# Reading a gate/up pair only when both are summed, with one w_down group between any two blocks

## The chip, the cores and the metric

The kernel runs on one core of a Trainium2 chip. The metric is the device time of one execution in microseconds (us), taken as the median of the runs. Engines are named as in the profile: PE multiplies matrices (PEld loads its stationary operand), DVE and ACT do elementwise work, POOL does a little of it, SP issues the transfers from memory.

## What is computed

One decoder layer on 256 tokens of width 2048, all in float32: a half-step feed-forward block, a mixer (sparse attention next to latent attention), and a second half-step feed-forward block. The change touches only the two feed-forward blocks:

```
def swiglu(x, w_gate, w_up, w_down):
    return (jax.nn.silu(x @ w_gate) * (x @ w_up)) @ w_down

h = rms_norm(x, ffn1_norm[l])
x = x + 0.5 * swiglu(h, ffn1_w_gate[l], ffn1_w_up[l], ffn1_w_down[l])
...
h = rms_norm(x, ffn2_norm[l])
x = x + 0.5 * swiglu(h, ffn2_w_gate[l], ffn2_w_up[l], ffn2_w_down[l])
```

w_gate and w_up are 2048 x 5632, w_down is 5632 x 2048.

## The kernel before

**Products.** Each float32 product is made of three products of a shorter format. A weight tile raw is split into w_hi (a rounding copy on ACT, line 470) and w_lo (a subtraction on DVE, line 478); mm3 (line 290) then issues high x high, high x low and low x high into the same sums.

**Parts.** Weights come as tiles of 1 MB, three of which can be in flight (RAW, line 28), and are split in parts of 1024 columns (the last part of a w_down tile has 512). Five parts may be split ahead of the one that PE is multiplying (SPLIT, line 28): the cast of a part can start when PE has finished with the part five places earlier, whose buffer it takes.

**Feed-forward work.** The 5632 hidden columns are 44 blocks of 128, in chunks of 6, 6, 6, 6, 6, 6, 4, 4 (CHS, line 22). A block is 96 matmuls of 256 columns: two parts of w_gate (q 0 and 1), two parts of w_up (q 2 and 3), 24 matmuls each. Gate goes to one half of a PSUM bank and up to the other half of the same bank (halves, line 650). Blocks of the first chunk take banks 4 and 5 in turn (ps_s); all later ones take bank 7 alone (ps_u, BANKS on line 30). A group of w_down products is called "D" in the plan: four parts, 7 x 3 = 21 matmuls of 512 columns into banks 0 to 6 (ps_m). It uses a scheme with seven products where eight would be direct, so DVE also adds weights (tsum, lines 461 to 466) and activations (lines 623 to 625). The groups of chunk k-1 are spread among the blocks of chunk k. The last chunk's w_down is multiplied directly after the last block ("L", ps_acc).

**Activation.** swish (line 591) takes a block from PSUM: DVE multiplies gate by the norm factor rb (ff_g), ACT takes tanh (ff_t), DVE finishes the silu (ff_g again) and multiplies by up, read from PSUM (asum). After every second block a pair is formed: three small DVE operations, a cast on ACT and a subtraction on DVE (act). Once all blocks of a chunk have met one half of w_down, the seven sums are added to a tile in SBUF (sum<-ps_m, turnover on line 653); after the last chunk but one, combine (line 667) folds them into x.

**Order.** Every engine runs its instructions in the order in which they were written out. go (line 212) writes that order at build time with a clock of its own for PE, DVE and ACT: dense work is one stream, and the activation steps are side jobs that step when their inputs are due by that clock. Waits between engines are put in from the tiles that each instruction reads and writes; a PSUM bank is one such tile. plan (line 331) sets how blocks and groups of w_down follow one another. Counted in PE's order, in chunks 1 to 5 and 7 a group of 21 matmuls stands before each block of 96. (Chunks are numbered from 0.) Chunk 6 has 4 blocks and 6 groups, and its matmuls between groups are 48, 72, 72, 48, 72, 72: two of its blocks follow another without a group between.

Of the kernel before, what the change touches and what calls it, by code (L numbers as in the profile page):

```python
# [7 lines left out]
F32 = mybir.dt.float32  # L8
# [6 lines left out]
P = 128  # L15
T = 256
# [6 lines left out]
FROM = [sum(CHS[:k]) for k in range(len(CHS))]  # L23
# [7 lines left out]
NEVER = 1e9  # L31
# [125 lines left out]
class _Layer:  # L157
# [32 lines left out]
        self.ev[key] = max([self.pe.clk] + [self.when(x) for x in aps])  # L190

    def at(self, *keys):
        return lambda: max(self.ev.get(k, NEVER) for k in keys)

    def fresh(self, *aps):
        return max(self.when(x) for x in aps)
# [134 lines left out]
    def plan(self):  # L331

        seq, way = [], 1
        for k, n in enumerate(CHS):
            gs = [("G", k, i, q) for i in range(0 if k else 2, n) for q in range(4)]
            if not k:
                seq += [("F", 0, 0, 0)] + gs
                continue
            ds = [("D", k - 1, g, j) for g in range(2)[::way] for j in range(CHS[k - 1] // 2)]
            way = -way  # L340
            for i, d in enumerate(ds):

                a, b = (len(gs) * x // len(ds) for x in (i, i + 1))
                if n >= len(ds):
                    a, b = (x // 4 * 4 for x in (a, b))
                seq.append(d)
                seq += gs[a:b]

        seq += [("L", LAST, 2 * g + i, q) for g in range(NG // 2) for q in range(CHS[LAST] // 2) for i in range(2)]
        return seq  # L350
# [234 lines left out]
    def ffn(self, ap, h, ssq, after, first):  # L585
        key, gain = ("f1", G_FFN1) if first else ("f2", G_FFN2)
# [4 lines left out]
        def swish(banks, pg, pu, k, i):  # L591

            n, (j, m) = FROM[k] + i, divmod(i, 2)
            yield self.at("rb" + key, *([("act", key, n - 2)] if n > 1 else []))
            yield self.fresh(pg)
            g, t = (ap.tile([P, T], F32, name=f"ff_{x}", tag=f"ff_{x}", bufs=2) for x in "gt")
            V.tensor_mul(g, pg, self.rb)
            S.activation(t, g, AF.Tanh, scale=0.5)
            yield self.fresh(t)
            V.scalar_tensor_tensor(g, t, 1.0, g, op0=ALU.add, op1=ALU.mult)  # L600
            yield self.at(("up", key, n), *([("act", key, n - 1)] if n else []))
            if m == 0:
                if n:
                    yield self.at(("pair", key, n // 2 - 1))
                raw[j] = ap.tile([P, 8, P], F32, name="asum", tag="asum")
            yield self.fresh(pu)

            r = raw[j]
            if k == LAST:
                dst = r[:, 2 * m:2 * m + 2]  # L610
            else:
                dst = r[:, 0:3:2] if m else r[:, 1:8:6]
            V.tensor_mul(dst, g.rearrange("p (a t) -> p a t", a=2), pu.rearrange("p (a t) -> p a t", a=2))
            self.leave(*banks)
            self.mark(("act", key, n), dst)
            if not m:
                return
            yield self.fresh(r)
            if k == LAST:
                f, r = acts[k][:, j, :, :4], r[:, :4]  # L620
            else:
                f = acts[k][:, j]
                V.tensor_sub(r[:, 3:5], r[:, 7:8].to_broadcast([P, 2, P]), r[:, 1:3])
                V.tensor_sub(r[:, 5], r[:, 1], r[:, 4])
                V.tensor_sub(r[:, 6], r[:, 0], r[:, 5])
                r = r[:, :7]
                yield self.fresh(r)
            S.copy(f[:, 0], r)
            yield self.fresh(f[:, 0])
            V.tensor_sub(f[:, 1], r, f[:, 0].bitcast(F32))  # L630
            self.mark(("form", key, k, j), f)
            self.mark(("pair", key, n // 2))
# [67 lines left out]
        def dense():  # L700
# [7 lines left out]
            for what, k, i, q in plan:  # L708
                if what == "F" or (what, i, q) == ("G", 0, 0):
                    acts[k] = ap.tile([P, 3, 2, 7, P], F32R, name="act", tag="act", bufs=2)  # L710
                if what == "F":
                    yield self.slot("acc", 4)
                    pb = [self.bank("acc")[:, :T] for _ in range(4)]
                    c = 0
                    while c < C:
                        yield self.at(*(("h", gain, x) for x in range(c, c + self.coming() // 512)))
                        w = self.take(P)
                        for j in range(w[0].shape[1] // 4):
                            for b in range(4):
                                self.mm3(pb[b], [x[:, 4 * j + b] for x in w], (h[:, c, 0], h[:, c, 1]), c == 0, c == C - 1)  # L720
                            c += 1
                            if j + 1 < w[0].shape[1] // 4:
                                yield
                        self.n_used += 1
                        yield
                    for b in range(2):
                        self.mark(("up", key, b))
                        self.spawn(swish(pb[2 * b:2 * b + 2], pb[2 * b], pb[2 * b + 1], 0, b))
                elif what == "G":
                    if q == 0:  # L730
                        yield self.slot("u" if k else "s", 1)
                        p = self.bank("u" if k else "s")
                    m, half = divmod(q, 2)
                    w = self.take(P)
                    for c in range(8):
                        cc = half * 8 + c
                        self.mm3(halves(p)[:, m], [x[:, c] for x in w], (h[:, cc, 0], h[:, cc, 1]), cc == 0, cc == C - 1)
                        if c in FINE:
                            yield
                    self.n_used += 1  # L740
                    yield
                    if q == 1:
                        self.spawn(swish([p], halves(p)[:, 0], halves(p)[:, 1], k, i))
                    if q == 3:
                        self.mark(("up", key, FROM[k] + i))
                elif what == "D":
                    if first and k == 0 and q == 0:
                        for g in (2 * i, 2 * i + 1):
                            self.fetch(self.columns(g), self.a["xt"][g])
                            self.mark(("x", g), self.columns(g))  # L750
                    new = q == 0 and (k == 0 or was[k, i][1] != i)
                    if new:
                        banks = {}
                    yield self.at(("form", key, k, q))
                    f = acts[k][:, q]
                    to = nxt.get((k, i))
                    end = q == CHS[k] // 2 - 1 and (to is None or to[1] != i)

                    for sums in (((1, 0), (6, 2)), ((0, 1), (3, 5)), ((4, 3), (5, 4)), ((2, 6),)):
                        if new:  # L760
                            for l, o in sums:
                                yield self.slot("m", 1)
                                banks[o] = self.bank("m")
                        w = self.take(512)
                        for j, (l, o) in enumerate(sums):
                            self.mm3(banks[o], (f[:, 0, l], f[:, 1, l]), [x[:, j] for x in w], new, end)
                        self.n_used += 1
                        yield
                    if end:
                        self.spawn(turnover(banks, k, i, (k, i) in began), 2)  # L770
                else:
                    if q == 0:
                        yield self.slot("acc", 2)
                        last[i] = [self.bank("acc"), self.bank("acc")]
                    p = last[i]
                    w = self.take(512)
                    yield self.at(("form", key, k, q))
                    f = acts[k][:, q]
                    for j in range(2):
                        for tb in range(2):  # L780
                            self.mm3(p[tb], (f[:, 0, 2 * j + tb], f[:, 1, 2 * j + tb]), (w[0][:, j], w[1][:, j]),
                                     q + j == 0, q + 1 == CHS[k] // 2 and j == 1)
                            if tb + j < 2:
                                yield
                    self.n_used += 1
                    yield
                    if q + 1 == CHS[k] // 2:
                        self.spawn(added(p, i))
# [786 lines left out]
```

## Time and profile before

| | us |
|---|---|
| median of 3 runs | 2023.28 (2023.16 to 2024.9) |
| the profiled execution | 2023.27 |
| its span, first to last instruction | 2021.5 |
| PE busy | 1865.4 (92%) |
| DVE busy | 1514.9 (75%) |
| ACT busy | 986.6 (49%) |
| first feed-forward block | about 0 to 830 |
| mixer | about 830 to 1225 |
| second feed-forward block | about 1225 to 2021 |

A row of the timeline gives start, length, engine, line, operation and tile, and in brackets the idle time before it and what ended that. Matmuls overlap, so a matmul's length is longer than the distance to the next one; the distance between starts is what counts. PEclk is the granted clock of PE, 1.00 at full rate. An execution is 1.77 us longer than its span.

### The profile page before, as it was taken

What the parts mean: (1) busy time and instruction counts of PE and PEld (TensorE: products, weight loads), DVE (VectorE), ACT (ScalarE), POOL (GpSimd) and SP (SyncE); (2) the same over time, 40 slices, a digit from 0 to 9 for tenths busy, and PEclk for the clock granted to TensorE, in tenths of its full rate; (3) what the DMA queues carried; (4) which work ended last, traced back from release to release, by engine and by line L of the source; (5) the groups of instructions that cost most, each with busy time, mean ns of one, the idle gap of its engine ahead of it and who ended that gap; (6) DMA issues with size and microseconds to landing.
All of it is one profiled execution on the core that took longest, in us unless ns stands there. A gap on an engine that the chain in (4) does not pass through costs nothing.

```text
span 2021.5 us, 30343 instructions
## 1 busy us (share of the span) xinstructions
PE 1865.4 (92%) x12157; PEld 1693.5 (84%) x12157; DVE 1514.9 (75%) x2272; ACT 986.6 (49%) x1289; POOL 101.0 (5%) x232
## 2 busy tenths in 40 slices
PE   7999999998999888899979999999989989999988
PEld 7988888888888788788867789898988888888887
DVE  7677777778777779776667765776778777778787
ACT  4454554444445444554555554454544544444442
POOL 6000000000000000101013200000000000000000
PEclk9999999999999899999989999999999999999999
DMA  6455554455445444475322454444554445445443
GB/s 234 171 195 194 179 193 153 163 188 177 157 167 185 148 176 158 158 269 207 130 97 85 148 186 167 167 175 159 188 188 167 167 167 188 166 154 182 166 167 125
DMA packets 54941, 344.29 MB, mean 170 GB/s; under 512 B 6544, under 2 KB 8592, under 8 KB 16912
## 3 DMA queue, kind: packets, MB, share of 16 engines
q1 hardware_dynamic: 54800, 342.36, 48.2%
q8 instruction: 95, 1.56, 0.3%
q14 instruction: 46, 0.38, 0.1%
HBM read 340.24 MB, written 2.10 MB: 169 GB/s over the span
## 4 chain that ended last, share of the span: by engine, by line
PE 68%; DVE 22%; issue 3%; ACT 3%; POOL 2%; DMA 1%; SPq 0%; ACTq 0%; POOLq 0%; DVEq 0%
PE ps_u L273 33%; PE ps_m L273 14%; PE ps_acc L273 12%; DVE w_lo L133 9%; PE ps_s L273 7%; DVE tsum L133 3%; ACT w_hi L133 2%; DVE ff_g L133 2%; DVE act L133 2%; DVE sum L133 2%; DVE asum L133 2%; DVE raw L133 1%; PE ps_t L273 1%; PE ps_t L288 1%; DVE x L133 1%
## 5 line engine op out<-in xcount | busy, mean ns | idle before, releaser
L273 PE MATMUL ps_u<-h,w_hi 128*128 128x256 f32 x4864 | 908.1, 289 | 106.0 <-DVE ff_g L133 103.5
L133 DVE TENSOR_TENSOR w_lo<-raw,w_hi 128x1024 fp32r<-128x1024 f32 (+4 forms) x645 | 773.8, 1215 | 256.0 <-ACT w_hi L133 254.8
L133 ACT CAST w_hi<-raw 128x1024 fp32r<-128x1024 f32 (+4 forms) x645 | 661.1, 1039 | 538.4 <-PE ps_u L273 199.4
L273 PEld LDWEIGHTS ps_u<-h,w_hi 128*128 128x128 f32 x4864 | 781.1, 196 | 128.3 <-DVE ff_g L133 118.0
L273 PE MATMUL ps_u<-h,w_lo 128*128 128x256 f32 x2432 | 698.5, 287 | 5.0 <-DVE w_lo L133 5.0
L273 PEld LDWEIGHTS ps_u<-h,w_lo 128*128 128x128 f32 x2432 | 477.4, 196 | 5.4 <-DVE w_lo L133 5.4
L273 PE MATMUL ps_m<-w_hi,act 128*128 128x512 f32 x1120 | 365.8, 396 | 0.0
L133 ACT CAST w_hi<-tsum 128x1024 fp32r<-128x1024 f32 (+1 forms) x160 | 133.4, 833 | 255.1 <-PE ps_u L273 226.6
L273 PEld LDWEIGHTS ps_m<-w_hi,act 128*128 128x128 f32 x1120 | 210.8, 188 | 47.7
L133 DVE TENSOR_TENSOR w_lo<-tsum,w_hi 128x1024 fp32r<-128x1024 f32 (+1 forms) x160 | 151.6, 953 | 111.0 <-ACT w_hi L133 111.0
L273 PE MATMUL ps_m<-w_lo,act 128*128 128x512 f32 x560 | 221.9, 396 | 0.0
L273 PEld LDWEIGHTS ps_m<-w_lo,act 128*128 128x128 f32 x560 | 105.3, 188 | 22.0
L273 PE MATMUL ps_acc<-w_hi,h 128*128 128x512 f32 (+2 forms) x384 | 119.8, 381 | 0.0
L133 DVE TENSOR_TENSOR tsum<-tsum,raw 128x512 f32<-128x512 f32 x160 | 109.2, 683 | 0.1
L133 ACT ACTIVATE ff_t<-ff_g 128x256 f32<-128x256 f32 x88 | 36.7, 420 | 134.1 <-DVE ff_g L133 134.1
L273 PE MATMUL ps_s<-h,w_hi 128*128 128x256 f32 x512 | 93.5, 285 | 4.2 <-DVE ff_g L133 4.2
L273 PEld LDWEIGHTS ps_s<-h,w_hi 128*128 128x128 f32 x512 | 80.0, 192 | 5.8 <-DVE ff_g L133 5.0
L273 PEld LDWEIGHTS ps_acc<-w_hi,h 128*128 128x128 f32 x384 | 71.2, 188 | 12.4 <-issue 1.6
L273 PE MATMUL ps_acc<-h,w_hi 128*128 128x256 f32 (+1 forms) x320 | 73.0, 317 | 5.4 <-ACT w_hi L133 5.0
L273 PE MATMUL ps_s<-h,w_lo 128*128 128x256 f32 x256 | 72.4, 283 | 0.0
L273 PE MATMUL ps_acc<-w_lo,h 128*128 128x512 f32 (+2 forms) x192 | 71.6, 373 | 0.0
L273 PEld LDWEIGHTS ps_acc<-h,w_hi 128*128 128x128 f32 x320 | 54.4, 200 | 8.6 <-ACT w_hi L133 5.0
(234 smaller groups left out, 1650.3 us busy)
## 6 DMA issues: line engine op xcount, KB each, us to landing
raw<-in_ffn_gate SPq DMA_DIRECT2D x84, 1024.0 KB, 4.8
raw<-in_ffn_up SPq DMA_DIRECT2D x84, 1024.0 KB, 4.8
raw<-in_ffn_down SPq DMA_DIRECT2D x80, 1024.0 KB, 4.8
raw<-in_w_out SPq DMA_DIRECT2D x16, 1024.0 KB, 4.8
raw<-in_ffn_rest SPq DMA_DIRECT2D x16, 512.0 KB, 3.4
raw<-in_w_q SPq DMA_DIRECT2D x8, 1024.0 KB, 4.7
raw<-in_w_cmp SPq DMA_DIRECT2D x4, 1024.0 KB, 4.9
raw<-in_w_sel SPq DMA_DIRECT2D x4, 1024.0 KB, 4.8
```

What stands on the lines that cost most here:

```text
L133: r = f(*args, **kw)
L273: self.nc.tensor.matmul(out, l, r, start=start, stop=stop)
L288: self.nc.tensor.transpose(out, src, self.ident if ident is None else ident)
```

## The change

Gate and up of a block are both read after the block's last matmul, no longer gate after the first half and up after the second. Up is no longer read by the DVE product but copied by ACT to a new SBUF tile ff_u, and the bank is given free right after the copy. plan puts exactly one group of w_down before each block; in chunk 6, which has two groups more than blocks, the two stand in the middle of a block, between gate and up.

```diff
@@ plan
-            for i, d in enumerate(ds):
-
-                a, b = (len(gs) * x // len(ds) for x in (i, i + 1))
-                if n >= len(ds):
-                    a, b = (x // 4 * 4 for x in (a, b))
-                seq.append(d)
-                seq += gs[a:b]
+
+            more = len(ds) - n
+            for i in range(n):
+                half = i * more // n < (i + 1) * more // n
+                seq.append(ds.pop(0))
+                seq += gs[4 * i:4 * i + 2]
+                if half:
+                    seq.append(ds.pop(0))
+                seq += gs[4 * i + 2:4 * i + 4]
+            assert not ds
@@ swish
-            yield self.fresh(pg)
-            g, t = (ap.tile([P, T], F32, name=f"ff_{x}", tag=f"ff_{x}", bufs=2) for x in "gt")
+            yield self.fresh(pg, pu)
+            g, t, u = (ap.tile([P, T], F32, name=f"ff_{x}", tag=f"ff_{x}", bufs=2) for x in "gtu")
             V.tensor_mul(g, pg, self.rb)
+            S.copy(u, pu)
+            self.leave(*banks)
             S.activation(t, g, AF.Tanh, scale=0.5)
             yield self.fresh(t)
             V.scalar_tensor_tensor(g, t, 1.0, g, op0=ALU.add, op1=ALU.mult)
-            yield self.at(("up", key, n), *([("act", key, n - 1)] if n else []))
+            yield self.at(*([("act", key, n - 1)] if n else []))
...
-            yield self.fresh(pu)
+            yield self.fresh(u)
...
-            V.tensor_mul(dst, g.rearrange("p (a t) -> p a t", a=2), pu.rearrange("p (a t) -> p a t", a=2))
-            self.leave(*banks)
+            V.tensor_mul(dst, g.rearrange("p (a t) -> p a t", a=2), u.rearrange("p (a t) -> p a t", a=2))
@@ dense
-                    if q == 1:
+                    if q == 3:
                         self.spawn(swish([p], halves(p)[:, 0], halves(p)[:, 1], k, i))
-                    if q == 3:
-                        self.mark(("up", key, FROM[k] + i))
```

**PE, a block of the first feed-forward block's second chunk.** The order with its waits, before, at the middle of the block (where the up half begins, 48 matmuls after its start):

```order
L273 MATMUL ps_u<-h,w_lo 128x256 [waits DVE_49]
L273 MATMUL ps_u<-h,w_hi 128x256 x2
L273 MATMUL ps_u<-h,w_lo 128x256
L273 MATMUL ps_u<-h,w_hi 128x256 [waits DVE_49]
```

and of the change, at the start of a block, behind the last matmul of the group of w_down:

```order
L273 MATMUL ps_m<-w_lo,act 128x512 [waits DVE_49]
L273 MATMUL ps_m<-w_hi,act 128x512
L273 MATMUL ps_u<-h,w_hi 128x256 [waits Activation_49]
L273 MATMUL ps_u<-h,w_hi 128x256
L273 MATMUL ps_u<-h,w_lo 128x256
```

The last row of the first piece, a wait of up's first matmul for DVE, is gone; no matmul in the middle of a block waits for the activation any more.

**DVE, around the end of a block of the same chunk** (w_lo<-raw are the next block's parts, w_lo<-tsum those of a w_down group). Before:

```order
L133 TENSOR_TENSOR ff_g<-ps_u,rb 128x256
L133 TENSOR_TENSOR w_lo<-tsum,w_hi 128x1024
L133 SCALAR_TENSOR_TENSOR ff_g<-ff_t,ff_g 128x256
L133 TENSOR_TENSOR w_lo<-tsum,w_hi 128x512
L133 TENSOR_TENSOR w_lo<-raw,w_hi 128x1024
```

```order
L133 TENSOR_TENSOR asum<-ff_g,ps_u 128x2x128
L133 TENSOR_TENSOR w_lo<-raw,w_hi 128x1024 x2
```

and of the change:

```order
L133 TENSOR_TENSOR w_lo<-tsum,w_hi 128x1024
L133 TENSOR_TENSOR w_lo<-tsum,w_hi 128x512
L133 TENSOR_TENSOR w_lo<-raw,w_hi 128x1024
L133 TENSOR_TENSOR ff_g<-ps_u,rb 128x256
L133 TENSOR_TENSOR w_lo<-raw,w_hi 128x1024
```

```order
L133 SCALAR_TENSOR_TENSOR ff_g<-ff_t,ff_g 128x256
L133 TENSOR_TENSOR asum<-ff_g,ff_u 128x2x128
```

The read of gate has moved to where the read of up stood: behind the subtraction of the next block's first part. On ACT the copy of up comes behind the casts of the next block's first two parts and waits for DVE:

```order
L133 CAST w_hi<-raw 128x1024 [waits PE_49,Activation_49]
L133 COPY ff_u<-ps_u 128x256 [waits DVE_49]
L133 ACTIVATE ff_t<-ff_g 128x256
```

**DVE, the end of a feed-forward block**, after the last block's read of gate, up to the act that the last w_down products wait for. Before:

```order
L133 TENSOR_TENSOR asum<-ff_g,ps_u 128x256
L133 TENSOR_TENSOR w_lo<-raw,w_hi 128x1024
L133 TENSOR_TENSOR sum_13736<-sum_13736 128x512 x3
L133 TENSOR_TENSOR sum_13736<-sum_13736 128x1024
L133 TENSOR_TENSOR w_lo<-raw,w_hi 128x1024
L133 TENSOR_TENSOR act<-asum,act 128x512
```

and of the change:

```order
L133 TENSOR_TENSOR ff_g<-ps_u,rb 128x256
L133 TENSOR_TENSOR w_lo<-raw,w_hi 128x1024
L133 TENSOR_TENSOR sum_13849<-sum_13849 128x512 x2
L133 SCALAR_TENSOR_TENSOR x<-sum_13849,rq,x 128x1024
L133 SCALAR_TENSOR_TENSOR ff_g<-ff_t,ff_g 128x256
L133 TENSOR_TENSOR asum<-ff_g,ff_u 128x256
L133 SCALAR_TENSOR_TENSOR x<-sum_13849,rq,x 128x1024
L133 TENSOR_TENSOR w_lo<-raw,w_hi 128x1024 x2
L133 TENSOR_TENSOR act<-asum,act 128x512
```

The whole silu of the last block now stands after its last matmul, with steps of combine among it.

In chunk 6 the matmuls between groups of w_down are now 96, 48, 48, 96, 48, 48 (each 48 a gate half or an up half), and every block has a group before it.

More of the change, by code (lines that the diff above doesn't have):

```diff
@@ L192, in at @@
     def at(self, *keys):
-        return lambda: max(self.ev.get(k, NEVER) for k in keys)
+        return lambda: max((self.ev.get(k, NEVER) for k in keys), default=0.0)
     def fresh(self, *aps):
@@ L726, in dense @@
                     for b in range(2):
-                        self.mark(("up", key, b))
                         self.spawn(swish(pb[2 * b:2 * b + 2], pb[2 * b], pb[2 * b + 1], 0, b))
```

## The prediction

> **What bounds the kernel now.** I read the page's busy times first, then the list of waits, then the timeline of PE.
>
> ```profile
> PE 1865.4 (92%) x12157; PEld 1693.5 (84%) x12157; DVE 1514.9 (75%) x2272; ACT 986.6 (49%) x1289; POOL 101.0 (5%) x232
> PE ps_u L273 <- DVE ff_g L133: 103.5, 72, 3.8
> PE ps_s L273 <- DVE ff_g L133: 4.2, 8, 0.6
> PE ps_u L273 <- DVE w_lo L133: 5.0, 2, 2.6
> DVE w_lo L133 <- ACT w_hi L133: 365.8, 282, 4.4
> ```
>
> PE is the busiest engine and its idle time has one large cause: 72 waits of up's first matmul for DVE's read of gate (ff_g). Gate and up share a bank. It almost never waits for weights (the w_lo row). The timeline shows where:
>
> ```profile
> 105.40 0.51 PE L273 MATMUL ps_u<-h,w_hi 128*128 128x256 f32 x2 [2.30 <-DVE ff_g L133]
> 122.35 0.50 PE L273 MATMUL ps_u<-h,w_hi 128*128 128x256 f32 x2 [0.51 <-DVE ff_g L133]
> 139.29 0.50 PE L273 MATMUL ps_u<-h,w_hi 128*128 128x256 f32 x2 [0.52 <-DVE ff_g L133]
> 411.52 0.50 PE L273 MATMUL ps_u<-h,w_hi 128*128 128x256 f32 x2 [0.52 <-DVE ff_g L133]
> 430.21 0.51 PE L273 MATMUL ps_u<-h,w_hi 128*128 128x256 f32 x2 [2.30 <-DVE ff_g L133]
> 431.73 0.63 PE L273 MATMUL ps_u<-h,w_hi 128*128 128x256 f32 x2
> 432.37 0.63 PE L273 MATMUL ps_u<-h,w_hi 128*128 128x256 f32 x2
> 434.93 0.48 PE L273 MATMUL ps_u<-h,w_hi 128*128 128x256 f32 x2
> 448.66 0.51 PE L273 MATMUL ps_u<-h,w_hi 128*128 128x256 f32 x2 [0.52 <-DVE ff_g L133]
> 632.96 0.51 PE L273 MATMUL ps_u<-h,w_hi 128*128 128x256 f32 x2 [0.52 <-DVE ff_g L133]
> 796.57 0.50 PE L273 MATMUL ps_u<-h,w_hi 128*128 128x256 f32 x2 [1.73 <-DVE ff_g L133]
> ```
>
> One wait per block, 0.52 or 2.30 us. The long ones come where DVE has other work ahead of the read (its rows of the same block):
>
> ```profile
> 427.01 1.08 DVE L133 TENSOR_TENSOR act<-asum,act 128x896 fp32r<-128x896 f32 x1
> 428.01 1.22 DVE L133 TENSOR_TENSOR w_lo<-raw,w_hi 128x1024 fp32r<-128x1024 f32 x1
> 429.14 0.68 DVE L133 TENSOR_TENSOR tsum<-tsum,raw 128x512 f32<-128x512 f32 x1
> 429.75 0.41 DVE L133 TENSOR_TENSOR ff_g<-ps_u,rb 128x256 f32<-128x256 f32 x1
> ```
>
> Many long waits cost twice. Matmuls come in threes (two high, one low). From 431.73 to 434.93 three take 0.64 us (432.37 - 431.73), elsewhere 0.35: near half rate for 3.2 us. Not every long wait does it: the period behind 105.40 has no such stretch and is as short as the next. The windows agree:
>
> ```profile
> 430.00:437.00 7.00, 6.79 (x43) 6.75 (x44) 2.32 (x4) 1.14 (x3) 0.00 (x0) 0.76 0.43 152
> 850.00:955.00 105.00, 105.00 (x548) 89.64 (x547) 74.44 (x127) 54.51 (x71) 10.33 (x29) 0.99 0.63 222
> ```
>
> The second row is the mixer: PE busy for all of 105 us at a granted 0.99, so unbroken work is not throttled here.
>
> What a block would take without waits: 48 matmuls of a gate half and 21 of a w_down group, start to start.
>
> ```profile
> 416.53 0.40 PE L273 MATMUL ps_m<-w_hi,act 128*128 128x512 f32 x1
> 421.45 0.39 PE L273 MATMUL ps_u<-h,w_hi 128*128 128x256 f32 x2
> 427.05 0.39 PE L273 MATMUL ps_u<-h,w_hi 128*128 128x256 f32 x2
> ```
>
> A half is 427.05 - 421.45 = 5.60 us, the group 421.45 - 416.53 = 4.92, so a block with its group is 2 x 5.60 + 4.92 = 16.12 us. Seen are 139.29 - 122.35 = 16.94 with a short wait (0.8 lost), 430.21 - 411.52 = 18.69 with a long one (2.6 lost), 448.66 - 430.21 = 18.45 where half rate follows (0.8 plus 1.5 lost).
>
> **The change part by part, steady stretch.** From 105.40 to 632.96 lie 29 block-and-group periods of chunks 1 to 5: 527.56 us against 29 x 16.12 = 467.5, so 60.1 lost, and 2.6 for the wait that ends at 105.40: 62.7. The second feed-forward block repeats it:
>
> ```profile
> 1296.96 0.51 PE L273 MATMUL ps_u<-h,w_hi 128*128 128x256 f32 x2 [2.30 <-DVE ff_g L133]
> 1824.71 0.50 PE L273 MATMUL ps_u<-h,w_hi 128*128 128x256 f32 x2 [0.51 <-DVE ff_g L133]
> 1987.74 0.50 PE L273 MATMUL ps_u<-h,w_hi 128*128 128x256 f32 x2 [1.74 <-DVE ff_g L133]
> ```
>
> 527.75 - 467.5 + 2.6 = 62.9. Together 125.6 us. Since the gate read no longer stands between matmuls of a block, all of it can go if nothing takes its place. The cover is the 4.92 us group of w_down ahead of the next block. Is the bank free by then? The same places in the old order:
>
> ```profile
> 416.66 1.05 ACT L133 CAST w_hi<-raw 128x1024 fp32r<-128x1024 f32 x1 [2.17 <-PE ps_u L273]
> 418.19 1.05 ACT L133 CAST w_hi<-raw 128x1024 fp32r<-128x1024 f32 x1 [0.48 <-PE ps_m L273]
> 417.74 1.22 DVE L133 TENSOR_TENSOR w_lo<-raw,w_hi 128x1024 fp32r<-128x1024 f32 x1 [2.53 <-ACT w_hi L133]
> 418.88 0.41 DVE L133 TENSOR_TENSOR asum<-ff_g,ps_u 128x256 f32<-128x256 f32 x1
> ```
>
> The up half ends at 416.5. The gate read will stand where asum stands, 418.88 to 419.29; the copy of up stands behind the two casts (the second ends at 419.24) and waits for the gate read. The copy's price is not in the trace; its neighbours are:
>
> ```profile
> L133 ACT COPY p_t<-ps_t 128x384 f32<-128x384 f32 x24 | 11.0, 480 | 3.3 <-PE ps_t L288 3.3
> L133 ACT ACTIVATE h<-ps_t,par 128x256 fp32r<-128x256 f32 x32 | 14.3, 473 | 12.8 <-DVE h L133 11.0 <-PE ps_t L288 1.7
> ```
>
> A copy of 384 columns takes 480 ns and a scaled read of 256 takes 473; the copy of 256 lies between 480 x 256/384 = 320 and 473, and I take 400. So the bank is free near 419.4 + 0.4 = 419.8, and PE wants it at 421.45: 1.6 us to spare. The 88 copies are 35 us of ACT, which is at 49%; uncovered they would add at most their own 0.4 us to each period. DVE does the same number of operations as before. Queued behind the copy are tanh and the casts of the next up parts. The third cast waits for the second part of the group (six matmuls, 6 x 0.234 = 1.4 us after the second cast, 419.6); behind copy and tanh it starts near 420.3, for a part that PE needs at 421.45 + 5.60. What is late next is nothing on PE's path.
>
> A rule of the Trainium skill bears on the half-rate term ("TensorE: Matmul & The Clock Gate", "HAM oscillation"): PE falls to half rate when idle gaps exceed about 3.4 us, a whole window of activity. The trace disagrees, since the 2.30 us wait before 430.21 was enough; by the rule alone those waits would cost only themselves. Counted by the rule, the steady stretch's gain would lack its half-rate share: of the 29 periods 12 end in a long wait and 17 in a short one, 12 x 2.6 + 17 x 0.8 = 44.8 of the 60.1 lost, so about 15 us less in each feed-forward block, an estimate.
>
> What may remain: DVE.
>
> ```profile
> 105.00:633.00 528.00, 491.22 (x3394) 457.50 (x3394) 400.75 (x515) 258.90 (x290) 0.00 (x0) 0.97 0.50 176
> 633.00:797.00 164.00, 147.15 (x981) 135.79 (x982) 134.15 (x173) 76.80 (x85) 0.00 (x0) 0.96 0.46 162
> L133 DVE TENSOR_TENSOR sum<-ps_m,sum 128x512 f32<-128x512 f32 x84 | 53.9, 679 | 0.0
> ```
>
> In the steady stretch DVE works 400.75 / 29 = 13.8 us per period; of 16.12 that is 86%, and the periods at 16.9 ran without a wait for w_lo. Three times per feed-forward block it adds seven sums more (7 x 0.68 = 4.8 us), which makes that period DVE-bound for about 2 us; five split parts ahead should hide most. I leave 5 us of waits per feed-forward block: kept gain 125.6 - 10 = **115.6**.
>
> **First chunk.** Four waits of about 0.5 us (the ps_s row: eight in all), 0.8 lost each, in both feed-forward blocks: 8 x 0.8 = **6.4** gained. Two banks in turn cover the reads there.
>
> **Chunks 6 and 7.** From 632.96 to 796.57 there are 8 blocks and 10 groups: 163.61 us against 8 x 11.20 + 10 x 4.92 = 138.8, so 24.8 lost; the second time 163.03, 24.2 lost. But DVE is busy 134.15 us of it, nearly all that PE would leave, since groups of w_down cost it weight sums and combine falls here. I expect half: **24.5** gained over both. The bounds are 0 and 49.
>
> **The end of each feed-forward block.** The last w_down products wait for the last act:
>
> ```profile
> 2000.29 0.74 PE L273 MATMUL ps_acc<-w_hi,act 128*128 128x512 f32 x2 [1.29 <-DVE act L133]
> L133 ACT ACTIVATE ff_t<-ff_g 128x256 f32<-128x256 f32 x88 | 36.7, 420 | 134.1 <-DVE ff_g L133 134.1
> L133 DVE SCALAR_TENSOR_TENSOR x<-sum,rq,x 128x1024 f32<-128x1024 f32 x8 | 10.1, 1282 | 0.1
> ```
>
> Now gate read, tanh and silu (3 x 0.42) come after the last matmul too, and in the order one 1024-wide step of combine (1.28) and one w_lo (1.2) more stand ahead of the act: 3.7 us longer, and PE has nothing else to do meanwhile. With the hops between engines I take 4 each, **8** lost over both. The bounds: 2, if combine is done earlier and only the silu is late; 14, with half rate and one more step after each.
>
> Sum: 115.6 + 6.4 + 24.5 - 8 = 138.5 less than the profiled execution's 2023.27, which is the median to 0.01: **1885 us**.
>
> **The rivals.** *All of it goes.* No new waits, chunks 6 and 7 at PE's pace, the end hidden: 125.6 + 6.4 + 49 = 181, so 1842 at best. For it: 86% DVE. Against it: 134 us of DVE in 139.
>
> *DVE sets the pace.* If each period keeps 3.0 us of DVE idling at the head of its queue (one such wait, at 417.74, is 2.53; the list has 365.8 us of them), a period is 13.8 + 3.0 = 16.8, 0.7 x 58 = 41 us lost instead of 10, and chunks 6 and 7 gain nothing: 1885 + 31 + 24.5 = 1940. For it: PE's stalls were slack for DVE too. Against it: consecutive 16.9 periods.
>
> *The wait only moves.* If DVE cannot run closer than now at all, PE's waits turn up at w_lo and the time stays within 4 us of 2023. Against it: the same 16.9 periods next to 18.7 ones with the same work.
>
> *Slower: the copy holds the bank.* ACT is served in order. Behind three more casts, two of which wait for the group's later parts (418.19 + 2 x 1.4 + 2 x 1.05 = 423.1), the copy would end near 423.5, PE would wait 2.0 us before each block, lose 2.3 with the restart and, at half rate after every second one, 0.7 more: 3.0 per block against 62.7/30 = 2.1 now, 0.9 x 60 = 54 us, with the end 8: about 2080. It decides once the copy starts over 6 us after up's end. Against it: the order puts it behind two casts, not five, about 3 us after up's end.
>
> **How the numbers follow.** Forecast 1885: 0.63. All goes (under 1862): 0.13. DVE sets the pace (1912 to 1960): 0.16. Only moves: 0.04. Copy holds the bank: 0.04. Faster by over 0.2% (4 us, about what a measurement here can tell from no change) are the first three, 0.92; the same 0.03, most of the fourth; slower 0.05. The range 1850 to 1930 leaves out the best of the second case, the worst of the third and the last two.
>
> **What would show it.** Right: no PE wait for ff_g in the middle of a block; ff_u waits under 5 us in total; block periods at 16.1 to 16.4 in chunks 1 to 5; PEclk 0.99 or more there. The end: PE's wait for act grown from 1.3 to about 5. Wrong: a row of PE waiting for ff_u or ff_g before each block (the copy's place), or many PE waits for w_lo (DVE), or matmul distances above 0.117 us at no wait (a clock that drops under unbroken work).

## The result, and the profile after

The changed kernel took 1864.01 us (median, 1863.02 to 1864.88), the kernel before on the same chip 2023.22 us. The ratio is 0.921, with an interval of 0.920 to 0.923: 159 us less, where 138.5 less (1885 us) was forecast. The time lies inside the forecast range.

The page's busy times, and from the list of waits those that the forecast spoke of (us in total, number, longest):

```profile
PE 1807.9 (97%) x12157; PEld 1648.9 (89%) x12157; DVE 1507.4 (81%) x2272; ACT 1001.4 (54%) x1377; POOL 100.7 (5%) x232
PE ps_acc L273 <- ACT act L133: 9.7, 2, 4.8
PE ps_acc L273 <- DVE act L133: 4.4, 2, 2.2
DVE w_lo L133 <- ACT w_hi L133: 233.9, 169, 4.2
ACT ff_u L133 <- DVE ff_g L133: 26.3, 11, 5.1
```

The 72 mid-block waits of PE for ff_g are gone, and PE has no wait for ff_u either. DVE does the same work in a shorter time; what shrank is its waiting for casts (365.8 us before, 233.9 now). ACT now waits 26.3 us for the gate read ahead of the copy, which PE does not feel. What grew is PE's wait for the last act: 1.3 us each before, now 4.8 and 2.2.

The timeline of PE between two blocks, and of DVE and ACT there (start, length, what, idle time before it):

```profile
297.73 0.40 PE L273 MATMUL ps_m<-w_hi,act 128*128 128x512 f32 x1
302.41 0.39 PE L273 MATMUL ps_m<-w_hi,act 128*128 128x512 f32 x1
313.85 0.40 PE L273 MATMUL ps_m<-w_hi,act 128*128 128x512 f32 x1
```

```profile
298.93 1.23 DVE L133 TENSOR_TENSOR w_lo<-raw,w_hi 128x1024 fp32r<-128x1024 f32 x1 [1.76 <-ACT w_hi L133]
300.07 0.42 DVE L133 TENSOR_TENSOR ff_g<-ps_u,rb 128x256 f32<-128x256 f32 x1
299.38 1.05 ACT L133 CAST w_hi<-raw 128x1024 fp32r<-128x1024 f32 x1 [0.48 <-PE ps_m L273]
300.53 0.37 ACT L133 COPY ff_u<-ps_u 128x256 f32<-128x256 f32 x1
300.80 0.42 ACT L133 ACTIVATE ff_t<-ff_g 128x256 f32<-128x256 f32 x1
```

A block ends at 297.73, where the next group of w_down begins; the next group begins at 313.85, 16.12 us later, the sum of the parts to the hundredth. The copy ends at 300.90, 3.2 us after the block, and PE wants the bank again behind the group's last matmul (302.41 + 0.23 = 302.64): 1.7 us to spare.

Windows over the same work: chunks 1 to 5, chunks 6 and 7, and the end of the first feed-forward block up to the mixer's first products of rc (us; busy time of PE, PEld, DVE, ACT, POOL; PEclk; DMA share; GB/s). Before:

```profile
96.60:643.00 546.40, 507.71 (x3512) 472.79 (x3511) 414.90 (x533) 267.58 (x299) 0.00 (x0) 0.97 0.50 178
643.00:801.60 158.60, 141.75 (x958) 131.36 (x957) 131.70 (x170) 73.72 (x81) 0.00 (x0) 0.96 0.47 166
801.60:847.00 45.40, 37.66 (x186) 29.65 (x184) 35.05 (x51) 24.96 (x45) 3.78 (x11) 1.00 0.43 154
```

After:

```profile
93.00:577.00 484.00, 484.00 (x3512) 454.91 (x3511) 410.94 (x532) 272.94 (x330) 0.00 (x0) 1.00 0.57 200
577.00:713.60 136.60, 135.25 (x960) 125.50 (x959) 129.99 (x169) 73.83 (x87) 0.00 (x0) 1.00 0.54 187
713.60:767.00 53.40, 39.78 (x187) 31.16 (x185) 37.72 (x56) 25.42 (x47) 3.85 (x11) 0.89 0.41 148
```

In the first row PE is busy for all of 484 us at a granted 1.00. In the second DVE is busy 130 of 136.6 us, and PE still hardly waits. In the third the time grew by 8.0 us and the clock fell.

Stage by stage, both feed-forward blocks together, between the same matmuls of both traces:

| | forecast | measured |
|---|---|---|
| first chunk (start of the first ps_u block: 96.64, then 93.08; second block 67.25, then 63.99) | 6.4 gained | 6.8 |
| chunks 1 to 5 (546.25 and 546.48, then 484.13 and 483.94) | 115.6 gained | 124.7 |
| chunks 6 and 7 (158.73 and 158.08, then 136.36 and 136.34) | 24.5 gained | 44.1 |
| the end (45.40 and 28.75, then 53.38 and 36.73) | 8 lost | 16.0 |
| mixer (373.92, then 374.85) | 0 | 0.9 lost |
| sum | 138.5 | 158.7 |

The sum is the difference of the two spans, 2021.5 - 1862.8.

### The profile page after: what moved, and what is told of

It reads as the page before. It is cut to its first block, busy times and chain, and to the rows that moved or that the text cites. A ratio compares the mean times of both kernels' runs of the same rounds, so it can differ in the third digit from the quotient of the medians.

```text
span 1862.8 us, 30489 instructions
## 1 busy us (share of the span) xinstructions
PE 1807.9 (97%) x12157; PEld 1648.9 (89%) x12157; DVE 1507.4 (81%) x2272; ACT 1001.4 (54%) x1377; POOL 100.7 (5%) x232
## 4 chain that ended last, share of the span: by engine, by line
PE 84%; DVE 10%; POOL 2%; issue 2%; ACT 1%; DMA 0%; SPq 0%; POOLq 0%; DVEq 0%; ACTq 0%
PE ps_u L273 41%; PE ps_m L273 18%; PE ps_acc L273 15%; PE ps_s L273 7%; DVE w_lo L133 5%; DVE sum L133 2%; PE ps_t L273 1%; PE ps_t L288 1%; POOL ssq L133 1%; DVE x L133 1%; POOL sqp L133 1%; DVE tsum L133 1%; POOL nw_t L133 0%; ACT w_hi L133 0%; DVE ff_g L133 0%
## 5 line engine op out<-in xcount | busy, mean ns | idle before, releaser
L273 PE MATMUL ps_u<-h,w_hi 128*128 128x256 f32 x4864 | 855.9, 279 | 0.0
L273 PEld LDWEIGHTS ps_u<-h,w_hi 128*128 128x128 f32 x4864 | 746.7, 188 | 7.3
L273 PE MATMUL ps_u<-h,w_lo 128*128 128x256 f32 x2432 | 680.0, 280 | 0.7 <-DVE w_lo L133 0.7
L273 PEld LDWEIGHTS ps_u<-h,w_lo 128*128 128x128 f32 x2432 | 457.0, 188 | 1.9 <-DVE w_lo L133 1.7
L273 PE MATMUL ps_acc<-w_hi,act 128*128 128x512 f32 x128 | 45.5, 430 | 15.5 <-ACT act L133 9.7
```

The lines of the kernel that those rows point to most:

```text
L273: self.nc.tensor.matmul(out, l, r, start=start, stop=stop)
```

## The experiments

**Each part alone.** The change has two parts, the order of groups and the reads. plan_alone puts only the new plan into the kernel before; read_alone keeps the old plan under the new reads.

```diff
@@ plan_alone: the kernel before, plan
+            more = len(ds) - n
+            for i in range(n):
+                ...
@@ read_alone: the changed kernel, plan
+            for i, d in enumerate(ds):
+                a, b = (len(gs) * x // len(ds) for x in (i, i + 1))
+                ...
```

> The old reads (gate in the middle of a block, up from PSUM by DVE) with the new order of blocks and groups of w_down. Theory (the reads set the time): chunks 1 to 5 keep their periods of 16.9 and 18.7 to 20.3 us; only chunk 6 gains, where 89 us were spent on 74 us of products: some 6 us in each feed-forward block, about 2011 us. Rival (the order of the groups did it): near 1890 us, periods of 16.1 us in chunks 1 to 5.

> The late reads and the copy with the old order, in which two blocks of chunk 6 follow another with no group between. Theory (the group of w_down covers the release of the bank, which takes some 3.3 us from up's end): chunks 1 to 5 at 16.12 us as in the whole change, and four waits of PE at the start of a block for the copy (ff_u), 3 to 4 us each, some with half rate after them: 1876 to 1886 us. Rival (the bank is free at once, the group covers nothing): no wait, 1864 us.

plan_alone took 2014.24 us (one time), read_alone 1877.48 (one time). So the reads bring 145 us by themselves, the plan 9 by itself, and some 13 on top of the reads. With the plan alone chunks 1 to 5 stay at 546.0 and 544.5 us, as expected, and PE's waits for ff_g stay:

```profile
PE ps_u L273 <- DVE ff_g L133: 103.0, 72, 4.7
```

With the reads alone chunks 1 to 5 run at 16.12 per period. What the plan is for shows in chunk 6, where a block follows another without a group between. read_alone, timeline of PE in chunk 6, first feed-forward block; the first and the last row are those places, the middle one lies within a block:

```profile
593.73 0.51 PE L273 MATMUL ps_u<-h,w_hi 128*128 128x256 f32 x2 [1.10 <-ACT ff_u L133]
617.87 0.58 PE L273 MATMUL ps_u<-h,w_lo 128*128 128x256 f32 x1 [2.42 <-DVE w_lo L133]
636.42 0.51 PE L273 MATMUL ps_u<-h,w_hi 128*128 128x256 f32 x2 [0.92 <-ACT ff_u L133]
```

Without the group PE waits for the copy's bank, though only about 1 us each, where 3 to 4 us were expected. These two waits are 2.0 of the 6.0 us that chunks 6 and 7 lose here (142.4 us, against 136.36), and 2.4 are the wait for w_lo. That the time came out as expected is in part luck.

**The copy.** no_copy reads both halves after up, but up by DVE's product straight from the bank, which is freed only after it.

```diff
...
-            S.copy(u, pu)
-            self.leave(*banks)
...
-            yield self.fresh(u)
+            yield self.fresh(pu)
...
-            V.tensor_mul(dst, ..., u.rearrange(...))
+            V.tensor_mul(dst, ..., pu.rearrange(...))
+            self.leave(*banks)
```

> Both halves are read after the last product, but up by DVE from PSUM as before; no copy on ACT. The bank is then free only after gate read, tanh, silu and asum, with one w_lo among them. From the old rows: gate read 2.4 to 2.8 us after up's end, w_lo to 3.9, silu to 4.4, asum to 4.8, with the hop about 4.9, just the 4.92 us of the group. Theory (the copy is what frees the bank in time): waits for asum of 0 to 1.5 us in many blocks, 1870 to 1930 us. Rival (late reading alone is enough): 1864 us or a little less, since ACT has 88 operations fewer.

1902.16 us (one time): the copy is worth 38 us. That is a balance: without it chunks 1 to 7 take 48 us more over both feed-forward blocks, and the two ends together 12.6 less. Waits and timeline of no_copy:

```profile
PE ps_u L273 <- DVE asum L133: 36.2, 18, 4.9
339.56 0.47 PE L273 MATMUL ps_u<-h,w_hi 128*128 128x256 f32 x2 [2.02 <-DVE asum L133]
725.74 0.76 PE L273 MATMUL ps_u<-h,w_hi 128*128 128x256 f32 x2 [4.90 <-DVE asum L133]
```

Most blocks still found the bank free: their periods are 16.1 to 16.3. The waits are fewer and longer than expected (18, 2.0 us on average) and gather where DVE is behind, at the turnovers (18.4 us) and in chunks 6 and 7 (150.27 us). The late read alone does most of the work. The copy still waits for the gate read, but what DVE and ACT do behind that (tanh, silu, the product) no longer keeps the bank.

**How near DVE is to the edge.** dve8 and dve4 add eight or four products of 256 columns (0.42 us each, where 0.36 was expected) on DVE behind each copy, into a tile that nothing reads.

```diff
             self.leave(*banks)
+            for _ in range(8):   # dve4: range(4)
+                z = ap.tile([P, T], F32, name="ff_z", tag="ff_z")
+                V.tensor_mul(z, self.rb, self.rb)
```

> The whole change, and in each block eight more DVE products of 256 columns into a tile that nothing reads (their output is left out of everything). Each costs 0.36 us back to back, 2.9 us per period. Theory (PE bounds, DVE has 16.12 - 13.8 = 2.3 us to spare per period): DVE becomes the bound at about 16.7 us, waits of PE for w_lo appear, about 1864 + 0.6 x 76 = 1910 us. Rival (DVE must idle some 2 us per period for its inputs): 18.7 us per period, about 2060 us. If DVE has more to spare than thought: 1864 us.

> The whole change, and four more DVE products of 256 columns in each block into a tile that nothing reads, 1.4 us per period: 13.8 + 1.4 = 15.2 of 16.12. Theory (DVE has 2.3 us to spare per period and can use nearly all of it): 1864 to 1870 us. Rival (DVE must idle for its inputs): 16.6 us or more per period, above 1895 us.

dve8 took 2123.55 us, more than both of its expectations, dve4 1917.88 (one time each). dve8, chunks 1 to 5 and two of the waits:

```profile
99.00:676.00 577.00, 516.37 (x3511) 477.50 (x3510) 507.75 (x769) 268.76 (x329) 0.00 (x0) 0.93 0.46 166
PE ps_m L273 <- DVE sum L133: 84.0, 8, 10.9
PE ps_m L273 <- DVE w_lo L133: 75.7, 31, 3.8
```

30 periods in 577 us are 19.2 on average, while DVE is busy 507.75 / 30 = 16.9. The average hides two kinds: the three at the turnovers take 29.3 each, the other 27 take 18.1 on average. PE waits for DVE in both, and the granted clock falls to 0.93 as well. dve4, chunks 1 to 5, and the timeline at a turnover:

```profile
92.00:590.00 498.00, 488.70 (x3516) 457.18 (x3515) 456.78 (x652) 272.26 (x330) 0.00 (x0) 0.99 0.55 195
```

```profile
332.35 1.79 DVE L133 TENSOR_TENSOR ff_z<-rb 128x256 f32<-128x256 f32 x4
334.06 1.88 DVE L133 TENSOR_TENSOR sum<-ps_m,sum 128x512 f32<-128x512 f32 x3
334.89 0.55 PE L273 MATMUL ps_m<-w_hi,act 128*128 128x512 f32 x1 [2.71 <-DVE sum L133]
```

The plain periods stay at 16.12 even with 1.7 us more on DVE. The three at the turnovers go to 20.59, 20.40 and 19.96: the extra products stand ahead of the last three of the seven sums, PE waits 2.71 us for one of the banks that these free, and half rate follows. That is 13 us in each feed-forward block; chunks 6 and 7 lose 11.9 and 13.7 more. The theory for dve4 missed. The time is where its rival put it (above 1895 us), but not by the rival's longer plain periods: there is room in a plain period, none at a turnover.

**The end.** It lost 16 us, and so was worth trying to mend. The changed kernel, DVE at the end of the first feed-forward block, and PE there:

```profile
715.18 3.39 DVE L133 TENSOR_TENSOR sum<-sum 128x512 f32<-128x512 f32 x4
718.49 0.42 DVE L133 TENSOR_TENSOR ff_g<-ps_u,rb 128x256 f32<-128x256 f32 x1
719.96 1.41 DVE L133 TENSOR_TENSOR sum<-sum 128x512 f32<-128x512 f32 x2
721.40 1.28 DVE L133 SCALAR_TENSOR_TENSOR x<-sum,rq,x 128x1024 f32<-128x1024 f32 x1
723.05 0.42 DVE L133 TENSOR_TENSOR asum<-ff_g,ff_u 128x256 f32<-128x256 f32 x1
```

```profile
713.57 0.39 PE L273 MATMUL ps_acc<-w_hi,act 128*128 128x512 f32 x1
724.18 0.79 PE L273 MATMUL ps_acc<-w_hi,act 128*128 128x512 f32 x1 [4.83 <-ACT act L133]
727.60 1.22 PE L273 MATMUL ps_acc<-w_hi,act 128*128 128x512 f32 x2 [2.20 <-DVE act L133]
729.04 1.05 PE L273 MATMUL ps_acc<-w_hi,act 128*128 128x512 f32 x2
```

Up ends at 713.57, and the gate read starts 4.9 us later, behind the rest of two subtractions (w_lo) and four sums of combine; three more steps of combine stand between it and asum. PE waits 7.0 us in two pieces, and what it multiplies from 724.18 to 731.6 runs at half rate. Two remedies were tried, alone and together: read the last block as before (early_last), or let combine's second half wait until the last pair has been formed (late_combine).

```diff
@@ early_last, swish
+            early = n == NF - 1
-            yield self.fresh(pg, pu)
+            yield self.fresh(pg) if early else self.fresh(pg, pu)
...
-            S.copy(u, pu)
-            self.leave(*banks)
+            if not early:
+                S.copy(u, pu)
+                self.leave(*banks)
...
@@ late_combine, combine
             yield self.fresh(s)
+            if g == 1:
+                yield self.at(("form", key, LAST, CHS[LAST] // 2 - 1))
```

> The whole change, but the very last block of each feed-forward block is read as before the change: gate after its half, up by DVE from PSUM. Theory (8 us at each end are lost because the silu of the last block comes after its last product): the two waits of PE for act at the end, 4.8 and 2.2 us, shrink to the 1.3 us of before, at the price of one mid-block wait of 1.7 to 2.3 us: 6 us gained at each end, about 1852 us. Rival (the end is long for another reason, combine): the silu is early but combine still stands in front of asum, 3 us or less gained at each end, 1858 us or more.

> The whole change, but combine of the second half of the columns may only be written out once the last block's act is formed. Theory (four sums of combine, 3.4 us, and two more steps stand in DVE's queue ahead of the last block's gate read and of its act): the read starts 2 us after up's end, not 4.9, the act is ready 5 us earlier, 10 us less in both ends: about 1854 us. Rival (silu itself sets the end): 1862 us or more. If combine, moved back, delays the last sums into x: above 1860 us.

> Both edits of the end together. If they cure the same wait: no better than the better one of them, 1850 to 1854 us. If they cure two: about 1846 us.

late_combine took 1852.44 us, ratio to the kernel before 0.916 (0.914 to 0.917), as expected; repeated, as late_again, 1853.79, 0.916 (0.915 to 0.918). The changed kernel, repeated beside other runs, was at 1864.98, 0.921 (0.919 to 0.924). late_combine, DVE and PE at the same place, and a window of 26.4 us there (PE busy 21.81; the changed kernel has 17.88 in it at a granted 0.81):

```profile
714.01 0.42 DVE L133 TENSOR_TENSOR ff_g<-ps_u,rb 128x256 f32<-128x256 f32 x1
719.23 0.68 DVE L133 TENSOR_TENSOR act<-asum,act 128x512 fp32r<-128x512 f32 x1
718.88 0.50 PE L273 MATMUL ps_acc<-w_hi,act 128*128 128x512 f32 x1 [0.69 <-ACT act L133]
727.73 0.50 PE L273 MATMUL ps_acc<-w_hi,act 128*128 128x512 f32 x1 [2.35 <-DVE x L133]
713.60:740.00 26.40, 21.81 (x98) 16.56 (x97) 21.84 (x30) 11.51 (x20) 0.00 (x0) 1.00 0.53 180
```

The gate read now starts 1.6 us after up's end (712.41), the act comes nearly in time and the clock stays up. Of the 11 us 5.3 lie in the second end (36.73 to 31.4), 3.5 in the first and 2.3 in the mixer. A wait of 2.35 us for x is new: the deferred combine now stands ahead of the adds that free ps_acc.

early_last took 1858.72 us, 0.919 (0.918 to 0.921), more than expected, and early_late 1863.37, 0.921 (0.920 to 0.923), not the sum of both but no gain at all. early_last, the middle of the last block, and its waits for act; then early_late's waits for x:

```profile
711.52 0.80 PE L273 MATMUL ps_u<-h,w_hi 128*128 128x256 f32 x2 [4.00 <-DVE ff_g L133]
PE ps_acc L273 <- DVE act L133: 1.6, 2, 1.1
```

```profile
PE ps_acc L273 <- DVE x L133: 7.0, 3, 2.4
```

In early_last both ends are back at 44.88 and 27.91 us, slightly below the kernel before, a gain of 8.5 and 8.8 where 6 each was expected: the 16 us come from reading the last block late. But DVE is 3.5 us behind when the gate half ends (its read starts at 711.05), so the old wait comes back there at 4.0 us with half rate behind it, and chunks 6 and 7 take 6.4 and 6.8 us more. That is dearer than the act waits of 0.69 and 0.35 which late_combine leaves at the first end. early_late pays the same price (6.7 and 5.8 us) and has almost no act wait left for the deferred combine to cure; what the deferral adds there is the wait for x, and its ends are 48.37 and 30.94.

**Deferring combine further.** later_combine lets its second half wait for the adds of the first two columns of x, so that these adds come first; late_later does that in the second feed-forward block alone and late_combine's in the first.

```diff
@@ later_combine, combine and turnover's last part
+            if g == 1:
+                yield self.at(("added", key, 1))
...
             self.leave(*ps)
+            self.mark(("added", key, g))
@@ late_later, combine
+            if g == 1 and first:
+                yield self.at(("form", key, LAST, CHS[LAST] // 2 - 1))
+            elif g == 1:
+                yield self.at(("added", key, 1))
```

> The whole change, with combine of the second half of the columns written out only when the first two of the four last sums have been added to x (late_combine let it go as soon as the act was formed, and PE then waited 2.35 us once at each end for a bank that the add behind combine had to free). Theory (DVE's order at the end is all that is lost there): that wait goes, the waits of 0.4 to 0.9 us for act stay, 2 to 3 us less at each end than late_combine: 1846 to 1849 us. Rival (combine, 7 us of DVE, then delays the last adds): 1852 us or more.

> The order of late_combine in the first feed-forward block, that of later_combine in the second, where no norm of a next phase stands behind the last adds. Theory (later_combine was slower only because its adds and norms delayed the way into the mixer; in the second block its end took 28.6 us against 31.4 in late_combine): 2.8 us less than late_combine, about 1849.5 us. Rival (the difference in the second end is chance): the same as late_combine.

later_combine took 1860.82 us, 0.920 (0.918 to 0.922), and missed its expectation. Its second end is 28.56 us as hoped, but the first is 51.8 and the mixer 380 (374.85 in the changed kernel), with this wait at the first end:

```profile
733.53 0.79 PE L273 MATMUL ps_acc<-w_hi,act 128*128 128x512 f32 x1 [3.27 <-DVE x L133]
```

Behind the first end the mixer needs x, and what is put off is missed there; why the mixer itself takes 5 us more was not followed up. late_later took 1850.58 us, 0.914 (0.913 to 0.916), as expected; its second end is 28.0 us. It is faster than the change by 13 us; against late_combine the intervals overlap.

## Why the prediction was right, and where it was off

**The steady stretch: right.** Both reads after up and the group of w_down as cover take the waits and their half rate away. The bank is free 3.2 us after up's end (worked out: about 3.3), the copy takes 0.37 us (0.40 was taken), and 1.7 us are to spare (1.6). The copy stands behind two casts, as the order had it, so *the copy holds the bank* falls; PE's waits for w_lo in ps_u and ps_m are 2.7 us in all, so *the wait only moves* falls too. plan_alone and no_copy show the parts: without the late read nothing is gained in these chunks, without the copy some comes back.

**5 us per feed-forward block for DVE at the turnovers: mis-sized.** Next to nothing remained: three periods of 16.2 to 16.4 among 30 of 16.12. dve4 shows how little it would take: 1.7 us more per period on DVE leave plain periods alone and cost each turnover 4 us. So the place was right, and the edge lies less than 1.7 us above the present load. *DVE sets the pace* describes dve8 rather than the change.

**Chunks 6 and 7, half of 49: mis-sized.** 44.1 came, 90%. (The waits for ff_g before are not all 0.52 or 2.30 us, as was read: the list's longest, 3.8, are here.) The step that failed took DVE's 134 us of work in a stretch of 139 as too much to run without new waits of PE. Between the matmuls that the stage table uses DVE has 131.70 us of work before and 129.99 after: it shed almost none, and its idle time went from 26.9 to 6.6 us without holding PE up. Nor was combine put off: the eight steps for its second half of the columns stand after the last matmul in both kernels. The margin is small: dve4 puts 13.5 us more on DVE in these eight blocks and loses 11.9 and 13.7.

**The end, 8: mis-sized, 16 measured.** The step counted what the order has behind the gate read. It missed that the four sums of combine, which stood behind that read before, stand ahead of it now. DVE in the kernel before, where up ends at 801.62:

```profile
796.11 0.41 DVE L133 TENSOR_TENSOR ff_g<-ps_u,rb 128x256 f32<-128x256 f32 x1
803.97 3.39 DVE L133 TENSOR_TENSOR sum<-sum 128x512 f32<-128x512 f32 x4
808.42 0.68 DVE L133 TENSOR_TENSOR act<-asum,act 128x512 fp32r<-128x512 f32 x1
```

So the read started 4.9 us after the last matmul, and the whole of combine's second half came ahead of the act, where only the four sums had before. Each end lost 8.0: the two act waits together 7.0 instead of 1.3, which is 5.7, and the remaining 2.3 is in the main half rate. late_combine, which takes only combine out of the way, brings 8.8 of the 16 us back at the two ends, net of the new wait for x. early_last, which reads early, brings all of it back there. So this cause is shown.

**The sum.** 158.7 came for 138.5. The steady stretch and chunks 6 and 7 gave 28.7 us more than their terms, the ends took 8.0 more than theirs; that the total is only 20 us off owes something to luck.

**Half rate.** The forecast counted its loss in full against the rule of the Trainium skill ("TensorE: Matmul & The Clock Gate", "HAM oscillation") that idle gaps beyond about 3.4 us bring it. The gain of 124.7 of the 125.6 us of losses bears that out: by the rule's count about 15 us less per feed-forward block would have been gained. dve4 gives the same answer: its 2.71 us wait is followed by matmuls of 512 columns 0.43 us apart instead of 0.23, at this granted clock (window behind that wait):

```profile
334.80:338.60 3.80, 3.71 (x9) 2.92 (x10) 3.77 (x7) 2.63 (x3) 0.00 (x0) 0.55 0.00 0
```

*All of it goes* came nearest of the rivals in chunks 1 to 7 (168.8 of its 174.6 us there), and failed at the end only.

## What to carry to other kernels

The Trainium skill ("PSUM — Partial Sum Buffer", "PSUM bank collisions raise a hardware error") asks that PSUM be guarded by bank and group of partitions, not by address; the order before agrees, where up's matmuls into the other half of the bank waited up to 3.8 us for the read of gate. When two results share a PSUM bank that is guarded as one tile, the reader of the first stalls the writer of the second; read both once, after the second, have matmuls into other banks between, and free the bank by the cheapest copy on the engine whose queue is short. A read that is moved later falls in behind whatever its engine has queued by then. That costs nothing where other work covers it and everything where none does, so look at the end of the stretch first and keep what nobody waits for out of the queue there. An average load (DVE busy 410.94 of 484 us, 85%, after the change) does not tell how near the edge is; the periods with the most work do.

## What the hardware showed that was not expected

Two things. Waits of 2 to 3 us brought half rate for 3 to 4 us, but not each one: 2.71 us in dve4 did; 2.02 us in no_copy did behind 538.91 and did not behind 339.56 (the next matmuls of 256 columns are 0.117 us apart); 2.30 us in the kernel before did at some places and not at others.

The trace of the kernel before shows a pattern in it: the half-rate stretches end on a raster of 3.41 us. Full rate comes back with these two rows and at 434.93, 544.14 and 581.65:

```profile
359.96 0.44 PE L273 MATMUL ps_u<-h,w_hi 128*128 128x256 f32 x2
397.42 0.48 PE L273 MATMUL ps_u<-h,w_hi 128*128 128x256 f32 x2
```

434.93 - 397.42 = 37.51 is 11 steps of 3.41, and 544.14 - 434.93 = 109.21 is 32 of them; the waits ahead of these stretches do not keep that step (393.03 and 430.21 are 37.18 apart). With the raster fitted to these ends, what decides is how much of a wait falls between two of its marks: between the first and the last ps_u matmuls of the two feed-forward blocks, none of the 12 waits of 1 us or more with at most 1.84 us there was followed by half rate, and all 26 with 1.96 us or more were. This was read from the trace afterwards, and no run was built to test it.

And an overloaded DVE cost more than its load: eight products more put 16.9 us of work on it per period, 0.8 over the 16.1, and the period grew by 3.1 on average, by 13.2 at each turnover and by 2.0 elsewhere.
